# Up-projection's head: first unit's fifth product tied behind the second unit's third; a weight step, squares and down-projection's differences issued later

## The chip, the cores and the metric
One Trainium2 chip, one of its cores. The kernel is one launch; its metric is the device time of the core in microseconds, lower is better. The profile is of one execution; its span runs from the first to the last instruction.

## The reference
One layer of a decoder block in float32 on x of 1 x 2048 x 1024:

```python
h = rmsnorm(x, attn_norm)
z = h @ w_in                      # pool channels | q | k | v | gates
a = pool_mixer(u_pool, w_pool, pool_scale)
b = swa_sink_attention(q, k, v, sinks)      # window 128
x = x + (g_pool * a + g_attn * b) @ w_out
h = rmsnorm(x, ffn_norm)
up = causal_depthwise_conv(h @ w_up, conv_w, conv_b)   # 1024 -> 2 * 2816, width 3
gate, val = up[..., :D_FF], up[..., D_FF:]
x = x + (silu(gate) * val) @ w_down
```

The change lies in the last four lines and in the output projection's sums for the second norm.

## The kernel before
The sequence is worked in two chunks of 1024 tokens (c = 0, 1): input projection and mixer, output projection (`Out`, `out_blocks`), up-projection (`Up`, `up`), down-projection (`Down`).

A product of f32 accuracy is made of fp32r matmuls: each factor is split into a rounded part and the rest (a ScalarE cast, L362 for weights and L1068 for activations, then a VectorE subtraction, L363 and L1069), and three of the four cross products are summed. On top of that the large projections use a scheme of seven block products in place of eight, with sums of blocks as factors (S1 to S4 of the weights, T1 to T4 of the activations).

In the up-projection, a unit f (22 of them, `u0`, `u1`, `u2`, ...) makes 128 gate and 128 value channels by seven products, methods `one` to `seven`. Each is 12 matmuls of 128x512 (`product`, L1254) into a bank of PSUM. A unit's `x` bank ("f" tag for u0 and u1) takes products one, three, five, seven in turn: after three, ScalarE copies the bank away (`kept`, L1444); after five, VectorE adds it to an earlier copy and writes half of the values (L1470); after seven, ScalarE copies it out (L1478). So five must wait for the copy, and seven for the add, of its own unit. Products four and six use another bank ("t" or "a"), and an add (L1474) ends six. Then come the convolution (L1489 on ScalarE, two L1492 on VectorE), SiLU (L1503), the gate's product (L1504) and a store.

The head of `up` handles units 0 to 2 together, because the factors T1 to T4 are only being made then: `right_t3`, `right_b22`, `right_t4` each subtract (L1237, L1247 for T4) and split. A unit's weights come in four steps (`weights(f, n)`): the second step holds L379, L382 and L383, the fourth L390 and L391.

The order on each engine is the scheduler's, from priorities by the place in the code; each engine works its queue strictly in that order. `with tc.issue_after(ins):` puts what is issued inside it right behind the instruction `ins` in that order, on ScalarE, VectorE and the others as well. It adds no dependence.

`Out.final` ends an output block: `added` (L1320) adds the residual, ScalarE squares the row (L1335), and VectorE adds the square to a sum (L1339). `stats` sums these sums over the channels by matmuls with a column of ones (L655), for the second norm. `Down.run` works through steps P1 to P7; for P2 it takes a difference of the loaded activations (L1888).

Of the kernel before, what the change touches and what calls it, by code (L numbers as in the profile page):

```python
# [21 lines left out]
ALU = mybir.AluOpType  # L22
# [200 lines left out]
def block_kernel(ctx: ExitStack, tc: tile.TileContext, x, xT, pos, vec, qkn, w_poolT, w_pool, w_q, w_kv,  # L223
                 w_gp, w_ga, w_out, w_up, w_down, outT):
    nc = tc.nc
    V, G, A = nc.vector, nc.gpsimd, nc.scalar
# [205 lines left out]
    for _ in range(20):  # L432
        nc.tensor.matmul(idle[:, 0:512], identr, identr.unsqueeze(1).to_broadcast([P, 4, P]),
                         start=True, stop=True)
# [815 lines left out]
    def product(bank, a, b, first):  # L1250
        i = 0
        for k in range(4):
            for x, y in ((0, 0), (0, 1), (1, 0)):
                nc.tensor.matmul(bank, a[:, x, k, :], b[k // 2][:, y, k % 2, :],  # L1254
                                 start=(first and i == 0), stop=(i == 11),
                                 skip_group_check=True)
                i += 1

    class Out:


        def __init__(self, c):
            self.c, self.m, self.w, self.b, self.xs, self.raws = c, [], [], {}, {}, []
            self.accs = [[], []]

        def mix(self):
            j = 3 - len(self.m)
# [49 lines left out]

        def added(self, h, n, m, bank):
            x = self.xs[h, n][:, m]
            V.scalar_tensor_tensor(x, bank, 0.5, x, op0=ALU.mult, op1=ALU.add)  # L1320

        def residual(self, h, n):
            x = self.xs[h, n] = up_.tile([P, 4, 512], F32, "U")
            load(x, self.rest(h, n))

        def final(self, h, n, m, bank):
            self.added(h, n, m, bank)
            x = self.xs[h, n][:, m]
            accs = self.accs[n]
            if not accs:  # L1330
                accs.append(fp.tile([P, 512], F32, "F"))
                A.square(accs[0], x)
            else:
                sq = mp.tile([P, 512], F32, "M")
                A.square(sq, x)  # L1335
                if h == 1 - n == 0 and m == 3:
                    accs.append(sq)
                else:
                    V.tensor_add(accs[0], accs[0], sq)  # L1339
            A.dma_start(x2d[4 * h + m][:, n * 512:n * 512 + 512], x)  # L1340

        def pairs(self):
# [3 lines left out]
    def out_blocks(ob):  # L1346

        heads = [Kept(f) for f in PRE]

        def run(*a, **kw):  # L1350
            for _ in ob.mul(*a, **kw):
                pass

        s = ps2.tile([P, T], F32, "s")
        x = [ps.tile([P, 512], F32, t) for t in "at"]
        x = [s[:, 0:512], x[0], s[:, 512:T], x[1]]
        ob.weights()
        ob.mix()
        ob.residual(0, 0)
        run(0, x, True, True)  # L1360
        ob.split()
        ob.first(2)
        right_t1(ob.m, ob.b, None)
        ob.mix()
        for m in range(4):
            ob.added(0, 0, m, x[m])
        ob.weights()
        ob.first(3)
        y = [ps.tile([P, 512], F32, t) for t in "ffta"]
        run(1, y, True, True)  # L1370
        ob.split()
        t2s = right_t2(ob.m, ob.b, None)
        ob.weights()
        for m in range(4):
            ob.final(0, 0, m, y[m])
        for n in ob.mul(2, x):
            if n == 0:
                ob.split()
                right_t3(ob.m, ob.b)
                ob.weights()  # L1380
            if n % 2 == 1:
                ob.kept(0, 1, n // 2, x[n // 2])
        for n in ob.mul(3, x):
            if n == 0:
                ob.split()
                right_t4(ob.m, ob.b, t2s)
                ob.weights()
                ob.residual(1, 0)
            if n % 2 == 1:
                ob.kept(1, 1, n // 2, x[n // 2])  # L1390
        for n in ob.mul(4, x):
            if n == 0:
                ob.split()
                ob.weights()
                right_b22(ob.m, ob.b)
            if n % 2 == 1:
                ob.final(1, 0, n // 2, x[n // 2])
        norms, b = [], {}

        def stats(n):  # L1400
            rstd(ob.accs[n], r2[:, 4 * n:4 * n + 4])

        def whole(n):
            return spread(r2[:, 4 * n:4 * n + 4], None)

        for n in ob.mul(5, y, True):
            if n == 0:
                ob.split()
                stream.fetch(stream.used + 1)
                stream.part(stream.used + 1)  # L1410
            if n == 2:
                stats(0)
            if n == 4:
                pb = whole(0)
            if n % 2 == 1:
                ob.final(1, 1, n // 2, y[n // 2])
        xg = ob.pairs()
        for j in range(2):
            right_first(xg, b, j, pb)
        for n in ob.mul(6, y):  # L1420
            if n % 2 == 1:
                ob.final(0, 1, n // 2, y[n // 2])
            if n == 3:
                for f in range(2):
                    heads[f].fetch("A11", "A12")
                stream.ahead().step(1)
        for j in range(2, 4):
            right_first(xg, b, j, pb)
        return xg, b, [lambda: stats(1), lambda: whole(1)], heads
# [3 lines left out]
    class Up:  # L1433
# [3 lines left out]
            self.c, self.f, self.b, self.w = c, f, b, w  # L1437

        def mul(self, bank, x, y, first=False):
            product(bank, self.w.w[x], self.b[y], first)  # L1440

        def kept(self, bank):
            t = qp.tile([P, 512], F32, "Q")
# [55 lines left out]
        def gate(self, yg=None):  # L1499
            if yg is None:  # L1500
                yg = self.conv(self.f, self.ug)
            t = mp.tile([P, T], F32, "M")
            A.activation(t, yg, AF.Silu)  # L1503
            V.tensor_mul(t, t, self.yv)  # L1504
            load(actd[self.f], t)

    def up(c, xg, b, norms, heads, dn):
        units = [Up(c, f, b, heads[f] if f < 2 else None) for f in range(FT)]

        def weights(f, n):  # L1510
            if f < FT:
                if units[f].w is None:
                    units[f].w = stream.get("up", f)
                units[f].w.step(n)

        u0, u1, u2 = units[:3]
        u0.one()
        norms[0]()  # L1520
        u1.one()
        pb = norms[1]()
        u0.two()
        weights(2, 0)
        u2.one("t")
        for u in (u0, u1):
            u.w.fetch("S1", "S4")
        u0.w.fetch("S3", "S2")
        right_t1(xg, b, pb)
        u1.two()  # L1530
        u2.two()
        t2s = right_t2(xg, b, pb)
        u0.four()
        u0.w.fetch("A22")
        u1.w.fetch("A22")
        right_t3(xg, b, (right_t2.sub, right_t2.low))
        third = parted.low
        u1.four("a")
        u0.three()
        last = Up.last  # L1540
        u1.w.fetch("S3", "S2")
        u1.three()

        with tc.issue_after(last):
            right_b22(xg, b)
        u0.five()
        with tc.issue_after(third):
            right_t4(xg, b, t2s)
        weights(2, 1)
        u0.six()  # L1550
        yg = u0.conv(0, u0.ug)
        u1.five()
        u0.seven()
        u0.value()
        weights(2, 1)
        u0.gate(yg)
        weights(2, 1)
        for f in range(2, FT + 1):
            u = units[f] if f < FT else None
            old = units[f - 1]  # L1560
            if u and f > 2:
                u.one()
                u.two()
            if f >= FT - 1:
                dn.fetch(3)
            weights(f + 1, 1)
            if u is None:
                old.six()
                dn.make(2)
                yg = old.conv(old.f, old.ug)  # L1570
                old.seven()
                old.value()
                old.gate(yg)
                break
            old.seven()
            old.value()
            weights(f + 1, 1)
            u.three()
            if f == FT - 1:
                dn.make()  # L1580
                if c + 1 < NCH:
                    spread(r1[:, c + 1, :])
            weights(f + 1, 1)
            old.six()
            if f < FT - 1:
                old.gate()
            weights(f + 1, 1)
            u.four()
            u.five()
            if f == FT - 1:  # L1590
                old.gate()
            if c + 1 < NCH and FT - 10 <= f < FT - 2:
                squares(c + 1, f - (FT - 10), row(c + 1, f - (FT - 10), fp, "F"))
            if c + 1 < NCH and f == FT - 2:
                norm1(c + 1, 0, NB)
# [198 lines left out]
    class Down:  # L1794
# [80 lines left out]
        def run(self, extra):  # L1875

            gives = []
            for i, (g, p, k) in enumerate(self.steps):
# [6 lines left out]
                        self.loads += [(1, int(p == "P4"), k, h) for h in range(2)]  # L1885
                if p == "P2":
                    a = self.raw[g, 0, k]
                    V.tensor_sub(a[:, 0:4:2], a[:, 1:4:2], a[:, 0:4:2])  # L1888
                if k > 0 and gives:
                    gives.pop(0)()  # L1890
                self.make(i + 1 + self.AHEAD - self.made)
# [255 lines left out]
```

## Time and profile before
| | |
|---|---|
| time, median of 3 runs | 2384.95 us (2383.26 to 2388.49) |
| the profiled execution, its own time | 2385.3 us |
| its span | 2383.6 us |
| mean granted TensorE clock | 0.998 |
| units' head, chunk 0 | about 603 to 630 us |
| units' head, chunk 1 | about 1768 to 1795 us |
| sums for the second norm, chunk 1 | about 1714 to 1729 us |
| start of down-projection, chunk 0 | about 1004 us |

The prediction quotes rows of several views. In the timeline a row is: start, duration, engine, line, operation, out<-in, shape, count, and in brackets the time that the engine sat idle before it and what ended that. A window's row has its length, each engine's busy time with its count, the granted TensorE clock, the share of the DMA engines and GB/s.

### The profile page before, as it was taken

The page shows a single profiled execution, that of the slowest core. Times are in us where ns is not written, and L with a number is a line of the kernel's source. Part 1 is how long each engine was busy: PE and PEld are TensorE (multiplying, and loading weights), DVE is VectorE, ACT ScalarE, POOL GpSimd, SP SyncE. Part 2 cuts the span into 40 slices and gives each one's busy share as a digit, 9 for nine tenths or more (in the row PEclk, how much of TensorE's full clock was granted, in tenths as well). Part 3 has the DMA queues.
Part 4 walks back from the last instruction along what each step waited for, and adds up shares of the span by engine and source line. Part 5 has one row for each costly group of instructions (what it writes and reads, how often), then busy time and mean ns, then how long its engine had stood idle before and what let it go on. Part 6 is the DMA issues. An engine that isn't in the chain of part 4 may idle for free.

```text
span 2383.6 us, 30120 instructions
## 1 busy us (share of the span) xinstructions
PE 2356.7 (99%) x11040; PEld 1958.7 (82%) x11040; DVE 1906.5 (80%) x2907; ACT 1185.7 (50%) x2164; POOL 190.5 (8%) x142
## 2 busy tenths in 40 slices
PE   9999999999999999999999999999999999999999
PEld 8888888888788888888888888888788888888887
DVE  8688888977977777899955867788798777779994
ACT  7555455455654555643623544455445545554441
POOL 1123121010000000000002232200000000000000
PEclk9999999999999999999999999999999999999999
DMA  9768778697222233644454776666733222228421
GB/s 348 241 202 237 223 213 286 216 344 270 73 88 91 93 106 106 210 168 162 133 195 151 228 219 196 197 207 230 234 129 105 80 80 80 80 75 288 141 71 53
DMA packets 165060, 408.10 MB, mean 171 GB/s; under 512 B 14128, under 2 KB 50480, under 8 KB 155184
## 3 DMA queue, kind: packets, MB, share of 16 engines
q1 hardware_dynamic: 151616, 373.48, 46.6%
q0 software_dynamic: 8256, 24.12, 4.3%
q10 hardware_dynamic: 5040, 8.58, 1.0%
q8 instruction: 87, 1.43, 0.2%
q14 instruction: 61, 0.50, 0.1%
HBM read 267.32 MB, written 138.81 MB: 170 GB/s over the span
## 4 chain that ended last, share of the span: by engine, by line
PE 85%; DVE 8%; DMA 3%; ACT 2%; issue 1%; POOL 0%; SPq 0%; DVEq 0%; ACTq 0%; POOLq 0%
PE f L1254 22%; PE f L266 16%; PE t L1254 12%; PE a L1254 6%; PE f L1912 4%; PE a L1912 4%; PE s L1912 4%; PE t L1912 4%; PE f L1098 3%; PE a L959 2%; PE s L898 2%; PE a L266 2%; PE t L931 1%; DVE U L1069 1%; DMA U<-xd 1%
## 5 line engine op out<-in xcount | busy, mean ns | idle before, releaser
L266 PE MATMUL f<-U,U 128*128 128x512 f32 (+1 forms) x2088 | 490.2, 389 | 4.5 <-ACT U L249 2.1
L266 PEld LDWEIGHTS f<-U,U 128*128 128x128 f32 x2088 | 381.3, 189 | 81.3 <-ACT U L249 2.7
L1254 PE MATMUL f<-U,U 128*128 128x512 f32 x1872 | 445.1, 390 | 2.7 <-ACT Q L1444 2.5
L1254 PEld LDWEIGHTS f<-U,U 128*128 128x128 f32 x1872 | 350.8, 188 | 77.7 <-ACT Q L1444 3.8
L1492 DVE SCALAR_TENSOR_TENSOR M<-F,vc,M 128x1024 f32<-128x1024 f32 x176 | 225.3, 1282 | 139.0 <-ACT M L1489 138.7
L1254 PE MATMUL t<-U,U 128*128 128x512 f32 x1332 | 314.6, 389 | 0.0
L1254 PEld LDWEIGHTS t<-U,U 128*128 128x128 f32 x1332 | 249.7, 188 | 52.4 <-ACT Q L1444 0.3
L362 ACT CAST U<-R 128x1024 fp32r<-128x1024 f32 x147 | 153.6, 1053 | 82.0 <-DVE R L391 42.6
L1254 PE MATMUL a<-U,U 128*128 128x512 f32 x756 | 183.9, 390 | 0.7 <-ACT Q L1444 0.7
L363 DVE TENSOR_TENSOR U<-R,U 128x1024 fp32r<-128x1024 f32 x147 | 179.2, 1221 | 0.3 <-ACT U L362 0.3
L1254 PEld LDWEIGHTS a<-U,U 128*128 128x128 f32 x756 | 141.3, 188 | 30.2 <-ACT Q L1444 1.2
L1254 PE MATMUL f<-U,M 128*128 128x512 f32 x624 | 150.2, 389 | 0.3 <-DVE F L1470 0.3
L917 ACT ACTIVATE Q<-s,st,rq 128x128 f32<-128x128 f32 x256 | 113.8, 456 | 49.9 <-DVE st L914 49.7
L1254 PEld LDWEIGHTS f<-U,M 128*128 128x128 f32 x624 | 117.0, 188 | 25.0 <-DVE F L1470 0.8
L939 POOL TENSOR_SCALAR_AFFINE_SELECT M<-M 128x1024 fp32r<-128x1024 f32 x64 | 94.4, 1475 | 383.4 <-DVE st L919 230.4
L1870 ACT CAST U<-U 128x1024 fp32r<-128x1024 f32 x76 | 79.0, 1051 | 84.7 <-PE s L1912 22.2
L1478 ACT COPY F<-f 128x512 f32<-128x512 f32 x52 | 30.5, 586 | 182.2 <-PE f L1254 182.0
L1489 ACT ACTIVATE M<-F,vc 128x1024 f32<-128x1024 f32 x88 | 109.4, 1243 | 3.3 <-DVE F L1474 1.9
L1871 DVE TENSOR_TENSOR U<-U,U 128x1024 fp32r<-128x1024 f32 x76 | 92.0, 1219 | 2.7 <-ACT U L1870 2.5
L1870 ACT CAST F<-U 128x1024 fp32r<-128x1024 f32 x44 | 46.2, 1049 | 93.8 <-PE a L1912 62.5
L966 ACT COPY U<-a 128x512 f32<-128x512 f32 x64 | 37.5, 586 | 108.5 <-PE a L959 108.3
L1098 PE MATMUL f<-U,U 128*128 128x512 f32 x384 | 88.5, 390 | 0.3 <-DVE M L1104 0.2
(320 smaller groups left out, 4051.9 us busy)
## 6 DMA issues: line engine op xcount, KB each, us to landing
R<-w_up SPq DMA_DIRECT2D x80, 512.0 KB, 3.7
actd<-M SPq DMA_DIRECT2D x44, 512.0 KB, 2.7
U<-w_down SPq DMA_DIRECT2D x88, 256.0 KB, 5.0
U<-actd SPq DMA_DIRECT2D x88, 256.0 KB, 5.2
qd<-U SPq DMA_DIRECT2D x64, 256.0 KB, 3.8
Q<-qd SPq DMA_DIRECT2D x64, 256.0 KB, 4.7
R<-w_out SPq DMA_DIRECT2D x30, 512.0 KB, 4.5
U<-kept_S SPq DMA_DIRECT2D x12, 1024.0 KB, 7.9
```

The costliest lines, as they stand in the source:

```text
L266: nc.tensor.matmul(out, a, b, start=(i == 0), stop=(i == n - 1))
L362: A.copy(t[:, 0], raw)
L363: V.tensor_sub(t[:, 1], raw, t[:, 0].bitcast(F32))
L917: A.activation(pr[:, h, :], sc[:, h, 0:P], AF.Exp, bias=nm[:, h:h + 1], scale=it["rq"][:, h:h + 1], accum_out=rs[:, h:h + 1])
L939: G.affine_select(own.rearrange("p a h q -> p (a h) q"), pa.bitcast(F32).rearrange("p a h q -> p (a h) q"), pattern=[[0, 8], [1, P]], base ...
L1098: nc.tensor.matmul(po, w[:, a, k, :], ms[k // 2][n][:, b, k % 2, :], start=(first and i == 0), stop=(last and i + 1 == len(order)))
L1254: nc.tensor.matmul(bank, a[:, x, k, :], b[k // 2][:, y, k % 2, :], start=(first and i == 0), stop=(i == 11), skip_group_check=True)
L1489: A.activation(y, u[:, 2:], AF.Identity, bias=cw[:, 3, m:m + 1], scale=cw[:, 2, m:m + 1])
L1492: V.scalar_tensor_tensor(y, u[:, j:j + T], cw[:, j, m:m + 1], y, op0=ALU.mult, op1=ALU.add)
L1870: A.copy(hi, src)
L1871: V.tensor_sub(lo, src, hi.bitcast(F32))
L1912: nc.tensor.matmul(into[m], u[:, 0, c_], v[:, 1], start=(first and j == 0), stop=(k == n - 1 and j == 2), skip_group_check=True)
```

## The change
Five edits, all of them to the order of issue:
1. u0's fifth product, with its add, is issued after the end of u1's third (`Up.end`).
2. u0's sixth follows the end of u0's fifth, and u1's sixth (issued in the loop, f == 2) the end of u0's sixth.
3. The step of u2's weights that holds L382 moves into the block that is issued after T3's last subtraction, with T4.
4. In `Out.final` a square's add is issued after the next block's L1320; `stats` issues what is left first.
5. Down-projection's differences of P2 are issued after the last gate's product.

```diff
+                ins = nc.tensor.matmul(bank, a[:, x, k, :], b[k // 2][:, y, k % 2, :],
+                                       start=(first and i == 0), stop=(i == 11),
+                                       skip_group_check=True).ins
...
+        return ins
...
         def final(self, h, n, m, bank):
-            self.added(h, n, m, bank)
+            with tc.issue_after(self.added(h, n, m, bank)):
+                while self.sums:
+                    self.sums.pop()()
...
                 else:
-                    V.tensor_add(accs[0], accs[0], sq)
+                    self.sums.append(lambda: V.tensor_add(accs[0], accs[0], sq))
...
         def stats(n):
+            while ob.sums:
+                ob.sums.pop()()
             rstd(ob.accs[n], r2[:, 4 * n:4 * n + 4])
...
         def mul(self, bank, x, y, first=False):
-            product(bank, self.w.w[x], self.b[y], first)
+            Up.end = product(bank, self.w.w[x], self.b[y], first)
...
-            V.tensor_mul(t, t, self.yv)
+            Up.gated = V.tensor_mul(t, t, self.yv).ins
...
         with tc.issue_after(last):
             right_b22(xg, b)
-        u0.five()
+        with tc.issue_after(Up.end):
+            u0.five()
         with tc.issue_after(third):
             right_t4(xg, b, t2s)
-        weights(2, 1)
-        u0.six()
+            weights(2, 1)
+        with tc.issue_after(Up.end):
+            u0.six()
+        six = Up.end
         yg = u0.conv(0, u0.ug)
         u1.five()
         u0.seven()
...
-            old.six()
+            with tc.issue_after(six) if f == 2 else nullcontext():
+                old.six()
...
                 if p == "P2":
                     a = self.raw[g, 0, k]
-                    V.tensor_sub(a[:, 0:4:2], a[:, 1:4:2], a[:, 0:4:2])
+                    with tc.issue_after(Up.gated):
+                        V.tensor_sub(a[:, 0:4:2], a[:, 1:4:2], a[:, 0:4:2])
```

Lines of the changed code lie up to 6 higher in `Up` (L1450 is the old L1444, L1476 the old L1470, L1480 the old L1474, L1498 the old L1492), 2 to 4 higher in `Out`.

The order on TensorE, at the head of chunk 0. f_5626 is u0's bank, f_5654 u1's, t_5767 that of u0's sixth; the right-hand factors are in the right place of each name pair.

```order
 L1254 MATMUL f_5626<-U_5764,U_5715 128x512 x6
+L1254 MATMUL f_5654<-U_5758,U_5823 128x512 x6
+L1254 MATMUL f_5654<-U_5764,U_5823 128x512 x6
 L1254 MATMUL f_5626<-U_5787,U_5715 128x512 x6
 L1254 MATMUL f_5626<-U_5791,U_5715 128x512 x6
-L1254 MATMUL t_5767<-U_5839,U_5711 128x512
-L1254 MATMUL a_5794<-U_5839,U_5713 128x512
-L1254 MATMUL t_5767<-U_5839,U_5711 128x512
-L1254 MATMUL f_5654<-U_5758,U_5823 128x512 x6
-L1254 MATMUL f_5654<-U_5764,U_5823 128x512 x6
-L1254 MATMUL t_5767<-U_5839,U_5711 128x512 x4
+L1254 MATMUL t_5767<-U_5839,U_5711 128x512 x6
```

u1's third stands ahead of u0's fifth now, and u0's sixth behind it in one piece. A little later, between u0's and u1's seventh, three matmuls of u2's third are left where twelve of it and eight of u1's sixth stood.

ScalarE at the same place; Q_5837 is the copy of u1's bank after its third product, U_5861 and U_5865 the two halves of T4, U_5868 the first weights of u2 to be split.

```order
 L1068 CAST U_5861<-U_4893 128x1024
-L1487 COPY uh_195<-F_5845 128x2
-L1444 COPY Q_5837<-f_5654 128x512
 L1068 CAST U_5865<-U_4894 128x1024
+L1450 COPY Q_5837<-f_5654 128x512
 L362 CAST U_5868<-R_5539 128x1024
 L362 CAST U_5924<-R_5537 128x1024
+L1493 COPY uh_195<-F_5845 128x2
```

The copy of u1's bank has moved behind the cast of T4's second half.

VectorE at the same place, before; F_5845 is u0's add after its fifth, F_5889 u1's, U_4894 the difference L1247 of T4's second half:

```order
L1069 TENSOR_TENSOR U_5842<-U_4894,U_5842 128x1024
L1470 TENSOR_TENSOR F_5845<-f_5626,Q_5780 128x512
L1069 TENSOR_TENSOR U_5861<-U_4893,U_5861 128x1024
L1247 TENSOR_TENSOR U_4894<-U_4894,M_5762 128x2x512
L1069 TENSOR_TENSOR U_5865<-U_4894,U_5865 128x1024
L363 TENSOR_TENSOR U_5868<-R_5539,U_5868 128x1024
```

and in the change:

```order
L1069 TENSOR_TENSOR U_5842<-U_4894,U_5842 128x1024
L1069 TENSOR_TENSOR U_5861<-U_4893,U_5861 128x1024
L1247 TENSOR_TENSOR U_4894<-U_4894,M_5762 128x2x512
L1069 TENSOR_TENSOR U_5865<-U_4894,U_5865 128x1024
L363 TENSOR_TENSOR U_5868<-R_5539,U_5868 128x1024
L1476 TENSOR_TENSOR F_5845<-f_5626,Q_5780 128x512
L363 TENSOR_TENSOR U_5924<-R_5537,U_5924 128x1024
L1480 TENSOR_TENSOR F_5624<-t_5767,Q_5821 128x512
L382 TENSOR_TENSOR R_5581<-R_5579,R_5581 128x512
L363 TENSOR_TENSOR U_5935<-R_5579,U_5935 128x1024
L1498 SCALAR_TENSOR_TENSOR M_5885<-F_5624,vc_129,M_5885 128x1024 x2
L1476 TENSOR_TENSOR F_5889<-f_5654,Q_5807 128x512
```

u0's add has moved behind four pieces of T4 and weight work. u1's add stands behind both of u0's conv rows L1498 for the gate channels.

VectorE at the sums of chunk 1, before; U_14585 and U_14593 are the blocks that the residual is added to, F_14470 the sum of squares, M_14716 the last square:

```order
L1320 SCALAR_TENSOR_TENSOR U_14585<-s_14308,U_14585 128x512
L382 TENSOR_TENSOR R_14734<-R_14732,R_14734 128x512
L1339 TENSOR_TENSOR F_14470<-F_14470,M_14665 128x512
L1320 SCALAR_TENSOR_TENSOR U_14585<-a_14309,U_14585 128x512
L1339 TENSOR_TENSOR F_14470<-F_14470,M_14682 128x512
```

and in the change:

```order
L1322 SCALAR_TENSOR_TENSOR U_14584<-s_14308,U_14584 128x512
L1343 TENSOR_TENSOR F_14470<-F_14470,M_14484 128x512
L1322 SCALAR_TENSOR_TENSOR U_14584<-a_14309,U_14584 128x512
L1343 TENSOR_TENSOR F_14470<-F_14470,M_14665 128x512
L1322 SCALAR_TENSOR_TENSOR U_14584<-s_14308,U_14584 128x512
```

L382 is gone from this place, and each L1343 adds the square of one block earlier.

More of the change, by code (lines that the diff above doesn't have):

```diff
@@ L1253, in product @@
             for x, y in ((0, 0), (0, 1), (1, 0)):
-                nc.tensor.matmul(bank, a[:, x, k, :], b[k // 2][:, y, k % 2, :],
-                                 start=(first and i == 0), stop=(i == 11),
-                                 skip_group_check=True)
+                ins = nc.tensor.matmul(bank, a[:, x, k, :], b[k // 2][:, y, k % 2, :],
+                                       start=(first and i == 0), stop=(i == 11),
+                                       skip_group_check=True).ins
                 i += 1
+        return ins
     class Out:
@@ L1264, in __init__ @@
             self.accs = [[], []]
+            self.sums = []
         def mix(self):
@@ L1319, in added @@
             x = self.xs[h, n][:, m]
-            V.scalar_tensor_tensor(x, bank, 0.5, x, op0=ALU.mult, op1=ALU.add)
+            return V.scalar_tensor_tensor(x, bank, 0.5, x, op0=ALU.mult, op1=ALU.add).ins
         def residual(self, h, n):
```

## The prediction
> **What bounds the kernel now.** I read the page first, then the list of waits of TensorE, then the timeline at each place where the change moves something, and last a table of windows for the clock. From the page:
>
> ```profile
> span 2383.6 us, 30120 instructions
> ...
> PE 2356.7 (99%) x11040; PEld 1958.7 (82%) x11040; DVE 1906.5 (80%) x2907; ACT 1185.7 (50%) x2164; POOL 190.5 (8%) x142
> ```
>
> The tensor engine TensorE (PE) is busy 99% of the span, and the change adds or removes no matmul. So only two things can change the time: gaps between matmuls, and the granted clock. The list of waits gives the gaps it can reach:
>
> ```profile
> engine line waited for: us in total, times, longest us
> ...
> PE f L1254 <- ACT Q L1444: 2.5, 2, 1.3
> PE a L655 <- DVE F L1339: 2.2, 1, 2.2
> ```
>
> The first is the up-projection's head, once in each chunk: TensorE waits for ScalarE's copy of a bank. The second is the row sums of squares in chunk 1. Here is the head of chunk 0 on the three engines:
>
> ```profile
> 603.71 3.21 PE L1254 MATMUL f<-U,U 128*128 128x512 f32 x12
> ...
> 607.56 0.58 ACT L1444 COPY Q<-f 128x512 f32<-128x512 f32 x1
> 608.04 3.16 ACT L1068 CAST U<-U 128x1024 fp32r<-128x1024 f32 x3
> 608.20 3.04 PE L1254 MATMUL f<-U,U 128*128 128x512 f32 x12 [1.27 <-ACT Q L1444]
> 608.83 1.22 DVE L1247 TENSOR_TENSOR U<-U,M 128x1024 f32<-128x1024 f32 x1
> 609.97 2.35 DVE L1069 TENSOR_TENSOR U<-U,U 128x1024 fp32r<-128x1024 f32 x2
> ...
> 612.24 0.68 DVE L1470 TENSOR_TENSOR F<-f,Q 128x512 f32<-128x512 f32 x1
> ...
> 614.67 0.59 ACT L1444 COPY Q<-f 128x512 f32<-128x512 f32 x1 [1.52 <-PE f L1254]
> 615.23 1.05 ACT L1068 CAST U<-U 128x1024 fp32r<-128x1024 f32 x1
> ...
> 616.74 2.88 PE L1254 MATMUL f<-U,U 128*128 128x512 f32 x12
> 617.45 1.22 DVE L363 TENSOR_TENSOR U<-R,U 128x1024 fp32r<-128x1024 f32 x1
> ...
> 619.46 2.88 PE L1254 MATMUL f<-U,M 128*128 128x512 f32 x12
> ...
> 622.65 0.69 DVE L382 TENSOR_TENSOR R<-R,R 128x512 f32<-128x512 f32 x1
> ...
> 623.25 2.47 DVE L1492 SCALAR_TENSOR_TENSOR M<-F,vc,M 128x1024 f32<-128x1024 f32 x2
> ...
> 630.11 5.15 PE L1254 MATMUL t<-U,U 128*128 128x512 f32 x22
> ...
> 988.53 2.60 DVE L1492 SCALAR_TENSOR_TENSOR M<-F,vc,M 128x1024 f32<-128x1024 f32 x2 [2.12 <-ACT M L1489]
> ```
>
> A product of 12 matmuls takes 2.72 us from start to start (616.74 to 619.46). u0's third, at 603.71, would be followed at about 606.76 (1.44 ahead of 608.20, counting what the wait's record leaves out, and after 0.2 and 0.1 of smaller gaps). VectorE (DVE) works without a pause here: its subtractions of 128x1024 follow each other by 1.14 (608.83 to 609.97), those of 128x512 by 0.60 (622.65 to 623.25), and two L1492 of which the second reads the first take 2.60 (988.53). That decides what follows.
>
> **Part 1, the head of chunk 0.** u1's third now fills 606.76 to 609.48, u0's fifth runs to 612.20, u0's sixth to 614.92. The old wait is gone. But three results that TensorE needs next have moved back behind the T4 work on ScalarE and VectorE (the order rows under the change), and I walk them with the durations above.
> - *u1's fifth* needs ScalarE's copy of u1's bank. It now stands behind the cast of T4's second half, which waits for the second subtraction L1247. On VectorE that one comes after 609.97 + 3 x 1.13 = 613.37 and ends at 614.59; the cast ends 1.05 later, at 615.69 with 0.05 to hand over; the copy, which overlaps it by 0.1 and takes 0.58, ends at 616.18. TensorE starts at 616.24 instead of 614.92: **1.3** of wait. Before, ScalarE did this copy at 614.67, ahead of that cast.
> - *u0's seventh* could start at 616.24 + 2.72 = 618.96. It needs u0's add L1470, before at 612.24. Ahead of it now stand L1069 (from 615.73), a cast that takes the buffer which this L1069 releases (616.99 to 618.04), and L363 (618.08); the add runs 619.22 to 619.91. TensorE starts at 619.97: **1.0**.
> - *u1's seventh* has three filler matmuls ahead and could start at 619.97 + 2.72 + 0.68 = 623.37. It needs u1's add, behind L363 (1.14), L1474 (0.60), L382 (0.60), L363 (1.14) and two dependent L1492 (2.56 to 2.60): from 619.82 that is 625.86, and the add ends at 626.55. TensorE starts at 626.61: **3.2**.
> - Then u1's seventh, nine and twelve matmuls: 626.61 + 2.72 + 2.04 + 2.72 = 634.09 for u2's fourth, which stood at 630.11. **Chunk 0: +4.0.** Behind it nothing new is late: the second part of the order is the old one, and VectorE has 24 matmuls to catch up.
>
> **Chunk 1** has the same queue:
>
> ```profile
> 1768.54 2.99 PE L1254 MATMUL f<-U,U 128*128 128x512 f32 x12
> 1772.80 3.04 PE L1254 MATMUL f<-U,U 128*128 128x512 f32 x12 [1.27 <-ACT Q L1444]
> ```
>
> Its order puts weight steps between the T4 work, and I count from the end of the cast that u1's copy waits for. u1's fifth starts 0.55 later, with a wait of 1.4. For u0's seventh VectorE does L1069 (1.14), L383, L390 and L391 (0.68, 0.61, 0.60), L363 (1.14) and the add (0.69), which ends 4.90 after the cast; TensorE could start at 0.55 + 2.72 = 3.27: 1.7. For u1's seventh follow L363, L1474, L363, L382, the two L1492 and the add, 1.14 + 0.60 + 1.14 + 0.60 + 2.56 + 0.69 = 6.7, against one product and four filler matmuls, 2.72 + 0.91: 3.0 (L363 starts with the product, within 0.1). In all 6.1, for the 1.5 that goes: **+4.6**. If VectorE were not late, both heads would lose their waits, 1.6 + 1.5 = -3.1; that is the lower end of this term, and +8.6 the upper.
>
> **Parts 2 and 3, the squares and the weight step in chunk 1.**
>
> ```profile
> 1714.27 1.23 POOL L1316 DMA_DIRECT2D U<-xT  x1 [5.24 <-issue]
> ...
> 1716.34 0.69 DVE L382 TENSOR_TENSOR R<-R,R 128x512 f32<-128x512 f32 x1 [4.71 <-DMA R<-w_up]
> ...
> 1718.93 0.69 DVE L1339 TENSOR_TENSOR F<-F,M 128x512 f32<-128x512 f32 x1 [0.70 <-ACT M L1335]
> ...
> 1723.66 1.05 PE L655 MATMUL a<-one,F 128*128 128x1 f32 x8 [2.16 <-DVE F L1339]
> ...
> 1726.31 2.76 PE L1298 MATMUL t<-U,U 128*128 128x512 f32 x6
> ```
>
> ```profile
> U<-xT POOLq DMA_DIRECT2D x4, 512.0 KB, 6.3
> ```
>
> VectorE stood 4.71 us at L382 for a DMA, and then each add waited for its square in turn (0.70 each round). With L382 behind the T4 work and each square's add behind the next L1320, VectorE follows the banks as TensorE fills them (one each 2.72): the last add of these sums ends about 1721.4, when TensorE gets there. That takes away about 2.3. One bound is the residual that GpSimd orders at 1714.27: 6.3 later is 1720.6, where L1320 wants it at about 1720.1, so I take **-2.1**.
>
> **The clock.**
>
> ```profile
> core 0: us, PE busy (x) PEld busy (x) DVE busy (x) ACT busy (x) POOL busy (x), PEclk, DMA share, GB/s
> 350.20:353.60 3.40, 1.50 (x5) 0.86 (x5) 3.40 (x6) 3.40 (x6) 0.00 (x0) 0.99 0.02 8
> 353.60:357.00 3.40, 3.15 (x8) 2.51 (x9) 3.40 (x9) 2.10 (x10) 1.13 (x1) 0.50 0.84 264
> 606.10:609.50 3.40, 2.13 (x10) 1.43 (x9) 3.40 (x4) 2.89 (x4) 0.00 (x0) 1.00 0.00 0
> 609.50:612.90 3.40, 3.40 (x17) 2.79 (x16) 3.40 (x5) 1.60 (x2) 0.00 (x0) 1.00 0.02 5
> ...
> 1722.30:1725.70 3.40, 2.04 (x13) 1.87 (x14) 1.46 (x3) 1.48 (x5) 0.70 (x1) 1.00 0.92 346
> 1725.70:1729.10 3.40, 3.40 (x11) 2.51 (x10) 1.72 (x3) 0.63 (x1) 0.34 (x1) 0.50 0.98 298
> ```
>
> Twice in the span the granted clock is 0.50 for 3.4 us, each time right behind a stretch with little matmul: 1.50 and 2.04 busy. The old head wait left 2.13, and the clock stayed at 1.00. One such stretch costs half of 3.4, **1.7**. The one at 1725.7 goes with the wait ahead of it: -1.7. But a wait of 3.0 to 3.2 us leaves, wherever such a stretch begins, one with at most about 1.8 busy. I therefore expect half a clock behind the third wait of each head, +1.5 each, since part of the wait falls into the slow stretch: together **+1.3**.
> [...]
>
> **Part 4, down-projection.**
>
> ```profile
> 994.37 1.23 DVE L1888 TENSOR_TENSOR U<-U 128x1024 f32<-128x1024 f32 x1 [2.10 <-DMA U<-actd]
> ...
> 1001.45 3.01 PE L1254 MATMUL f<-U,M 128*128 128x512 f32 x12 [0.35 <-DVE F L1470]
> ...
> 1006.38 0.97 PE L1912 MATMUL f<-U 128*128 128x512 f32 x3 [0.56 <-ACT F L1478]
> ```
>
> At the end of chunk 0's up-projection VectorE stands 2.10 in front of a difference, L1888, until its operand lands, and TensorE then waits twice, 0.35 and 0.56 by the record, 1.2 with the matmuls' starts. The differences now come behind the last gate, so the add L1470 no longer stands behind them: **-1.2**. They are read only by down-projection's fourth group of steps, some 15 us later, which covers the delay; uncovered it would be one difference, 1.2. Chunk 1 has no wait there.
>
> **Sum** on the profiled 2385.3 (span 2383.6 and 1.7 around it; 0.35 above the median of the runs): +4.0 + 4.6 - 2.1 - 1.2 + 1.3 = +6.6, 2391.9; against the median, and rounded, **2391.6**.
>
> **Rivals.**
> - *The clock stays* behind the new waits. [...] Against: the two rows above. 2391.6 - 3.0 = **2388.6**.
> - *Half the waits*: ScalarE and VectorE work some 1 us ahead of my walk, each wait halves, and no clock drops. Heads 2.8 - 1.6 and 3.0 - 1.5, the rest -2.1 - 1.7 - 1.2: 2385.3 - 2.3 - 0.3 = **2382.7**. For it: a walk over twenty instructions adds its errors up. Against: each handover in it is a row's duration.
> - *The other side: faster.* VectorE gets ahead of TensorE, because u1's third in front gives it 2.72 us. It decides at u0's add: if that runs by 616, u0's seventh never waits and u1's add follows in time. Heads -3.1, sums -2.1, clock -1.7, down -1.2: -8.1, **2377**. Against it: VectorE is busy 3.40 of 3.40 in both windows of the old head, so 2.72 us of other matmuls create no room, and the order puts its adds later than before.
>
> **Chances.** Forecast 0.52 (one drop only would still be 2390); clock stays 0.20; half the waits 0.10; faster 0.13; worse than forecast 0.05 (the residual late, or the drop of chunk 1's squares staying too). The bounds of the unknown terms (0.5 on the squares, 0.7 on each head's walk, 1.7 on the clock) reach 2394; the lower end takes in the rival of the clock and that of half the waits, 2382. About 0.2% of the time, 4.8 us, is what a measurement of this kernel can tell from no change: below 2380.2 is faster, above 2389.7 slower. Faster 0.14, within 0.32, slower 0.54.
>
> **What would show it.** In the changed kernel's timeline: three waits of TensorE in each head (copy, u0's add, u1's add) near 1.3, 1.0 to 1.7 and 3.1; the record of L655 without a wait; no wait at the first row of L1912's kind; windows with clock 0.50 just behind u1's seventh. I am wrong if u1's add ends before TensorE wants it, or if the clock never drops in a head.

## The result, and the profile after

| | before | changed |
|---|---|---|
| median, same chip | 2384.46 us (6 runs, 2380.28 to 2388.49) | 2397.03 us (6 runs, 2391.52 to 2403.17) |
| ratio, 95% interval | | 1.0055 (1.0038 to 1.0071) |
| the profiled execution | 2385.3 us | 2400.55 us |
| a second series, with a second profile | 2384.21 us (17 runs) | 2394.63 us (4 runs), 1.0042 (1.0028 to 1.0056) |

The change makes the kernel slower: by 0.55% in the first series and by 0.42% in the second. The direction was forecast; the size was not: 2391.6 with a range up to 2394 was given.

The engines' busy times from the page of the changed kernel, and its list of waits of TensorE (in all, times, longest):

```profile
PE 2362.6 (98%) x11040; PEld 1962.7 (82%) x11040; DVE 1907.3 (80%) x2907; ACT 1185.5 (49%) x2164; POOL 190.3 (8%) x142
```

```profile
PE f L1254 <- DVE F L1476: 10.0, 4, 4.7
...
PE a L655 <- DVE F L1343: 2.5, 1, 2.5
PE f L1254 <- ACT Q L1450: 2.4, 2, 1.2
```

TensorE has the same number of matmuls. A new first row stands in the list: 10.0 us for VectorE's adds of the fifth products, in four waits. The other two rows have nearly the numbers of before, but they are other waits: the copy waited for is now that of u1's bank, no longer that of u0's, and the wait at L655 is at a later place, as will be seen.

The head of chunk 0, and the three waiting products of chunk 1, in the changed kernel's timeline:

```profile
603.20 8.66 PE L1254 MATMUL f<-U,U 128*128 128x512 f32 x36
...
615.13 0.58 ACT L1450 COPY Q<-f 128x512 f32<-128x512 f32 x1
...
615.76 3.04 PE L1254 MATMUL f<-U,U 128*128 128x512 f32 x12 [1.18 <-ACT Q L1450]
...
618.74 0.68 DVE L1476 TENSOR_TENSOR F<-f,Q 128x512 f32<-128x512 f32 x1
...
619.48 3.01 PE L1254 MATMUL f<-U,M 128*128 128x512 f32 x12 [0.68 <-DVE F L1476]
...
622.64 0.69 DVE L382 TENSOR_TENSOR R<-R,R 128x512 f32<-128x512 f32 x1 [1.49 <-DMA R<-w_up]
...
627.08 0.69 DVE L1476 TENSOR_TENSOR F<-f,Q 128x512 f32<-128x512 f32 x1
...
627.83 4.60 PE L1254 MATMUL f<-U,M 128*128 128x512 f32 x12 [4.66 <-DVE F L1476]
...
637.03 3.33 PE L1254 MATMUL t<-U,U 128*128 128x512 f32 x14
...
1788.18 3.02 PE L1254 MATMUL f<-U,U 128*128 128x512 f32 x12 [1.19 <-ACT Q L1450]
...
1792.62 3.03 PE L1254 MATMUL f<-U,M 128*128 128x512 f32 x12 [1.42 <-DVE F L1476]
...
1799.83 5.49 PE L1254 MATMUL f<-U,M 128*128 128x512 f32 x12 [3.27 <-DVE F L1476]
```

The three waits of each head are there, for the three instructions that the prediction names. The second is a little shorter than forecast, and the third of chunk 0 is 4.66 by its record, 4.8 counted from the starts of the matmuls: 1.6 more than the 3.2 forecast. The reason stands a few rows above it: VectorE stood 1.49 us at L382 for a load. The product behind the wait lasts 4.60 in place of 2.9, which is the clock. The windows show it:

```profile
624.71:628.12 3.41, 0.29 (x1) 0.29 (x2) 2.92 (x3) 0.94 (x4) 0.00 (x0) 1.00 0.00 0
628.12:631.53 3.41, 3.41 (x9) 2.68 (x9) 2.26 (x2) 3.38 (x3) 0.00 (x0) 0.50 0.00 0
1747.70:1751.11 3.41, 1.14 (x6) 0.60 (x4) 3.41 (x5) 1.99 (x3) 0.00 (x0) 1.00 1.01 339
1751.11:1754.52 3.41, 3.17 (x15) 3.20 (x16) 1.41 (x3) 1.75 (x4) 0.00 (x0) 0.50 0.98 372
1754.52:1757.93 3.41, 3.41 (x10) 2.73 (x11) 1.72 (x3) 0.17 (x1) 1.01 (x1) 0.50 0.90 317
1795.48:1798.90 3.42, 1.08 (x5) 0.56 (x3) 3.10 (x3) 0.10 (x1) 0.00 (x0) 1.00 0.44 144
1798.90:1802.31 3.41, 2.48 (x6) 2.00 (x7) 2.03 (x3) 3.19 (x4) 0.00 (x0) 0.50 0.00 0
1802.31:1805.72 3.41, 3.41 (x10) 2.64 (x9) 2.54 (x3) 1.43 (x3) 0.00 (x0) 0.50 0.00 0
```

The clock drops behind the third wait of each head, as forecast, but in chunk 1 it stays down for two windows, and for two more it drops at 1751, where nothing was forecast. That makes five windows of 3.41 at half clock, at up to 1.7 each (a little less in the two in which TensorE was busy for only 3.17 and 2.48); the kernel before had two such windows. What happened ahead of 1751:

```profile
1713.81 1.23 POOL L1318 DMA_DIRECT2D U<-xT  x1 [8.68 <-ACT U L1284]
...
1723.17 1.23 POOL L1318 DMA_DIRECT2D U<-xT  x1 [8.14 <-issue]
...
1723.92 1.47 SPq L243 DMA_DIRECT2D U<-kept_A  x2
...
1736.73 0.69 DVE L1322 SCALAR_TENSOR_TENSOR U<-t,U 128x512 f32<-128x512 f32 x1 [4.18 <-DMA U<-xT]
...
1751.35 0.56 PE L655 MATMUL a<-one,F 128*128 128x1 f32 x2 [2.51 <-DVE F L1343]
```

The norm's sums are taken twice in a chunk, once for each half of the columns. The first (1727.05) had no wait left, as forecast. The second waits 2.51 here: VectorE stood 4.18 for the last piece of the residual, which GpSimd ordered at 1723.17 and which landed 13 us later, beside two loads of 1024 KB that SyncE ordered at 1723.92.

### The profile page after: what moved, and what is told of

It is laid out like the page before. It is cut to its first block, busy times and chain, and to the rows that moved or that the text cites. A ratio compares the mean times of both kernels' runs of the same rounds, so it can differ in the third digit from the quotient of the medians.

```text
span 2398.8 us, 30131 instructions
## 1 busy us (share of the span) xinstructions
PE 2362.6 (98%) x11040; PEld 1962.7 (82%) x11040; DVE 1907.3 (80%) x2907; ACT 1185.5 (49%) x2164; POOL 190.3 (8%) x142
## 4 chain that ended last, share of the span: by engine, by line
PE 85%; DVE 9%; DMA 2%; ACT 2%; issue 1%; POOL 0%; DVEq 0%; SPq 0%; ACTq 0%; POOLq 0%
PE f L1254 22%; PE f L266 16%; PE t L1254 12%; PE a L1254 6%; PE f L1923 4%; PE a L1923 4%; PE s L1923 4%; PE t L1923 4%; PE f L1098 3%; PE a L959 2%; PE s L898 2%; PE a L266 2%; DVE U L1069 1%; PE t L931 1%; PE s L1300 1%
## 5 line engine op out<-in xcount | busy, mean ns | idle before, releaser
L1498 DVE SCALAR_TENSOR_TENSOR M<-F,vc,M 128x1024 f32<-128x1024 f32 x176 | 225.6, 1282 | 151.9 <-ACT M L1495 151.2
```

The lines of the kernel that those rows point to most:

```text
L1498: V.scalar_tensor_tensor(y, u[:, j:j + T], cw[:, j, m:m + 1], y, op0=ALU.mult, op1=ALU.add)
```

## The experiments

Each ran beside the kernel before on the same chip; the first four share runs of before (median 2384.56 us, 25 runs), the other four as well (2384.21 us, 17 runs). "Parts" are the five edits of the change. One sentence of the text ahead has to be put right first: a tie acts on the engine of the instruction that is named, not on all. `issue_after(Up.end)` holds matmuls; the adds and copies were not tied, and moved because the scheduler put other work of their engines first.

**Parts 1 and 2 alone**

```diff
-        u0.five()
+        with tc.issue_after(Up.end):
+            u0.five()
...
-        u0.six()
+        with tc.issue_after(u0.end5):
+            u0.six()
+        six = Up.end
...
-            old.six()
+            with tc.issue_after(six) if f == 2 else nullcontext():
+                old.six()
```

> Only parts 1 and 2 of the change (u0's fifth behind u1's third, the sixths tied), all else as before. Theory (the ties alone bring the adds and the copy behind T4 and weight work): three waits of TensorE in each head, about 1.3, 0.9 and 4.7 in chunk 0 (the third with L382's wait for its load, 1.5), about 1.4, 1.6 and 3.0 to 3.4 in chunk 1, half clock behind the third; the old wait of 2.2 at L655 for the first sums stays, none at the second L655. Time 8 to 12 us above before, about 2394. Rival (the loss comes from the moved weight step and the squares): the third wait of chunk 0 stays under 3.3 without a wait at L382, and the time lies within 5 us of before.

Measured: 2399.48 us, ratio 1.0058 (1.0041 to 1.0075). Its waits:

```profile
PE f L1254 <- DVE F L1471: 11.3, 5, 4.6
...
PE f L1254 <- ACT Q L1445: 1.7, 2, 1.1
...
PE a L655 <- DVE F L1340: 0.9, 1, 0.9
```

Two rows of its timeline:

```profile
623.19 0.69 DVE L382 TENSOR_TENSOR R<-R,R 128x512 f32<-128x512 f32 x1 [1.38 <-DMA R<-w_up]
...
1738.20 0.69 DVE L1321 SCALAR_TENSOR_TENSOR U<-t,U 128x512 f32<-128x512 f32 x1 [3.60 <-DMA U<-xT]
```

The two head ties alone cost 15 us, which is all of the loss and more than the 8 to 12 expected. L382 waits for its load ahead of u1's add in chunk 0 without part 3, too, so part 3 didn't bring it there. The second half of the expectation failed: the wait at the first sums, which was to stay without part 4, had gone (VectorE stood 1.82 at L382 there, where it had stood 4.71), and two waits of 0.9 stood at the second sums, where none was expected. VectorE stood 3.60 for the late residual here too, so the order of the squares isn't needed for that.

**Parts 4 and 5 alone, and parts 3 to 5**

```diff
             with tc.issue_after(self.added(h, n, m, bank)):
                 while self.sums:
                     self.sums.pop()()
...
                     with tc.issue_after(Up.gated):
                         V.tensor_sub(a[:, 0:4:2], a[:, 1:4:2], a[:, 0:4:2])
```

> Only parts 4 and 5 (squares' adds one block later, down-projection's differences behind the last gate); the head and the weight step as before. Theory: head waits as before (one of 1.3 in each chunk), down-projection's two waits gone (-1.2), L655's first wait smaller than before's 2.2. If the residual's transfer collides with other loads because of part 4's order, a second L655 wait of about 2.5 with half clock shows here too, and the time is 2384 to 2388; if it needs the head's delay or the moved weight step, there is none and the time is about 2380.

> Parts 3, 4 and 5, without the head's ties. Theory: as e2, with L382 out of the squares of chunk 1, so the first L655 wait is under 0.5 and no half clock stands behind it: 2379 to 2381 if the second L655 does not wait, 2384 to 2387 if it does. The second L655 wait here but not in e2 would put it on the moved weight step; in both, on the squares; in neither, on the ties or on chance. Rival (parts 3 to 5 gain nothing): the time equals before within 1 us.

Measured: 2380.20 us, ratio 0.9986 (0.9977 to 0.9995), and with part 3 2380.40, 0.9989 (0.9979 to 0.9998). Of the waits that the change is concerned with, parts 4 and 5 leave only the old ones of the heads:

```profile
PE f L1254 <- ACT Q L1450: 2.5, 2, 1.3
```

So squares and differences gain some 4 us, close to the 2.1 + 1.2 + 1.7 (clock behind the first sums) forecast for them. Part 3 adds nothing that can be measured to that. With parts 4 and 5 alone VectorE still stands 3.64 us at L382 for its load in that stretch, but the adds of the squares then catch up before TensorE asks for the sum.

**The ties, with the adds held in front** (parts 1, 2, 4, 5; T4's second subtraction behind u0's add, u1's fifth behind u0's sixth)

```diff
-            right_t4(xg, b, t2s)
-            weights(2, 1)
+            right_t4(xg, b, t2s, sum0)
+        weights(2, 1)
...
-        u1.five()
+        with tc.issue_after(six):
+            u1.five()
```

> Parts 1, 2, 4 and 5, and one more tie: T4's second subtraction L1247 is issued behind u0's add L1470, and u1's fifth behind u0's sixth. The order then has u0's add ahead of T4's second half, u1's copy ahead of its cast, and fourteen filler matmuls between the sevenths. Theory (the loss is the late copy and adds, not u1's third in front): chunk 0's head keeps at most one wait of 0.5, chunk 1's has 0.9 and 2.1; no half clock in chunk 0. Time about 2380 to 2384. Rival (u1's third in front costs by itself, whatever the adds do): waits in chunk 0 of over 3 in all and a time above 2390.

Measured: 2381.78 us, ratio 0.9991 (0.9981 to 1.0000). The waits for the adds:

```profile
PE f L1255 <- DVE F L1477: 2.1, 2, 1.8
...
PE f L1255 <- DVE U L1069: 0.7, 1, 0.7
```

The time lies in the 2380 to 2384 expected, and chunk 0's head keeps one wait, of 0.33. So u1's third product in front need not cost much: with u0's add ahead of T4's second half again, and more matmuls between the sevenths, 15 us shrink to 1.6 over parts 4 and 5 alone. The loss comes from where adds and copy stand relative to the products that need them. This run doesn't part the two remedies: it puts the adds earlier in VectorE's order, and it also has fourteen matmuls between the sevenths where the changed kernel has three, which alone give u1's add 2.5 us more (11 x 2.72 / 12).

**The changed kernel once more**

> The changed kernel once more, unaltered, for a second profile. Theory A (the residual's second half lands late by the order of the transfers itself): the second row sums of squares in chunk 1 wait about 2.5 us for VectorE's add again, the last of GpSimd's residual transfers is issued over 9 us after the one before, and two stretches of half clock follow. Theory B (chance of one execution): that transfer is issued 6 to 7 us after the one before, there is no such wait, and the profiled time is about 6 us lower than the first profile's 2400.55. Either way the three waits of chunk 0's head stay within 0.3 of 1.3, 0.8 and 4.8. Median 2395 to 2399.

Measured: 2394.63 us, just under the 2395 to 2399 expected; profiled execution 2394.95. Rows of its timeline and windows:

```profile
628.42 4.61 PE L1254 MATMUL f<-U,M 128*128 128x512 f32 x12 [4.65 <-DVE F L1476]
...
1714.84 1.23 POOL L1318 DMA_DIRECT2D U<-xT  x1 [8.44 <-DMA R<-wo_g]
...
1723.45 1.23 POOL L1318 DMA_DIRECT2D U<-xT  x1 [7.38 <-ACT M L1339]
...
1733.86 0.69 DVE L1322 SCALAR_TENSOR_TENSOR U<-t,U 128x512 f32<-128x512 f32 x1
...
1750.00 0.28 PE L655 MATMUL a<-one,F 128*128 128x1 f32 x2
```

```profile
1792.81:1796.22 3.41, 0.89 (x4) 0.76 (x5) 2.33 (x3) 1.62 (x3) 0.00 (x0) 1.00 0.05 18
1796.22:1799.63 3.41, 3.41 (x10) 2.63 (x9) 2.84 (x3) 2.64 (x3) 0.00 (x0) 0.50 0.00 0
```

Theory B holds in the main: the heads' waits are the same within 0.03 (1.35, 0.82, 4.82 in chunk 0, counted from matmul starts), but no wait stands at the second sums, and the clock drops for one window behind each head. So 5.6 us of the first profile's loss belonged to that execution. Theory B's detail was wrong: the last order went out 8.6 us after the one before, not 6 to 7. What differed was the landing. In the first profile the order's packets start at 1728.46, after those of the two loads from kept_A (1725.42), and end at 1736.22; here they start at 1725.39, ahead of the loads' (1729.24), and end at 1730.24. In these two profiles the transfer whose packets came first was done first; why the order of the packets differs isn't shown.

**The residual in four orders** (chunk 1's last two quarters)

```diff
-            if m % 2 == 1:
-                m = slice(m - 1, m + 1)
+            one = h == self.c == 1
+            if m % 2 == 1 or one:
+                m = slice(m if one else m - 1, m + 1)
                 G.dma_start(x[:, m], self.rest(h, n)[:, m], accum_op=ALU.add)
```

> The changed kernel; only in chunk 1, the residual of the last two 512-column quarters is added by four orders of 256 KB from GpSimd, one for each bank, where there were two of 512 KB. Theory (each 512 KB order waits until the one before has landed): with quarters the last order goes out at about 1716 to 1718 instead of 1723.2, all has landed by about 1727, the second row sums of squares wait less than 0.7 us and the two half-clock stretches behind them go: 5 to 6 us below the changed kernel, about 2391. Rival (the loads from SyncE take the DMA engines, whoever is issued when): the last quarter lands after 1733 still, the wait stays above 1.5 us, and the time is within 2 us of the changed kernel's.

Measured: 2397.40 us, ratio 1.0050 (1.0037 to 1.0064).

```profile
1714.63 1.75 POOL L1319 DMA_DIRECT2D U<-xT  x2 [7.78 <-ACT U L1284]
1718.09 0.88 POOL L1319 DMA_DIRECT2D U<-xT  x1 [1.71 <-ACT U L1315]
...
1719.09 3.03 PE L1300 MATMUL s<-U,U 128*128 128x512 f32 x12 [1.46 <-DVE U L1323]
...
1750.64 0.28 PE L655 MATMUL a<-one,F 128*128 128x1 f32 x2
```

The mechanism held and the gain did not come. The last order goes out at 1718.09, as expected, its packets have ended at 1725.53, and the second sums have no wait. But the time is no lower than the changed kernel's two medians, 2397.03 and 2394.63: another wait, 1.46 at the bank of L1300, stands where the changed kernel had 0.3 to 0.6, since a weight load from wo_g came later, and in this profile chunk 0's head took two windows at half clock. How often the late residual strikes in unprofiled runs isn't known; this run doesn't show that it sets the median.

**The fourth weight step later** (what VectorE does of it held behind u1's add)

```diff
+        sum1 = Up.sum
         u0.seven()
         u0.value()
-        weights(2, 1)
+        with tc.issue_after(sum1):
+            weights(2, 1)
```

> The changed kernel; only VectorE's and, through it, ScalarE's work of unit 2's fourth weight step is held behind unit 1's add in the up-projection's head. That takes L363, L382 (which stood 1.49 us for its load in the changed kernel) and L390 from between unit 0's add and unit 1's. By durations alone the waits of chunk 0's head become 0.6, 1.0 and 2.3, those of chunk 1 1.4, 0.5 and 3.8. If the third wait of chunk 0 was 4.8 because of L382's wait for its load, it falls to 2.3, chunk 0 gains 3.0 to 3.5 and its half-clock stretch may go too (another 1.7). If it was 4.8 because VectorE's queue is slower than the sum of its durations, it falls by the removed work alone, to about 3.9, and chunk 0 gains about 2. Median 2391 to 2394 by the first, 2394 to 2396 by the second.

Measured: 2392.23 us, ratio 1.0030 (1.0018 to 1.0042). Timeline of the head of chunk 0, and windows:

```profile
620.60 0.69 DVE L1476 TENSOR_TENSOR F<-f,Q 128x512 f32<-128x512 f32 x1
...
623.29 2.61 DVE L1498 SCALAR_TENSOR_TENSOR M<-F,vc,M 128x1024 f32<-128x1024 f32 x2 [1.41 <-ACT M L1495]
626.00 0.69 DVE L1476 TENSOR_TENSOR F<-f,Q 128x512 f32<-128x512 f32 x1
...
626.75 3.04 PE L1254 MATMUL f<-U,M 128*128 128x512 f32 x12 [2.16 <-DVE F L1476]
```

```profile
622.82:626.24 3.42, 1.77 (x8) 1.13 (x6) 2.81 (x3) 0.69 (x3) 0.00 (x0) 1.00 0.00 0
626.24:629.65 3.41, 2.90 (x13) 2.38 (x14) 3.15 (x5) 3.27 (x5) 0.00 (x0) 1.00 0.18 36
1786.77:1790.18 3.41, 1.38 (x7) 0.80 (x5) 2.81 (x3) 1.07 (x1) 0.00 (x0) 1.00 0.52 154
1790.18:1793.59 3.41, 1.28 (x3) 1.09 (x4) 3.16 (x5) 1.99 (x4) 0.00 (x0) 0.50 0.00 0
1793.59:1797.00 3.41, 3.41 (x9) 2.65 (x9) 3.17 (x3) 2.27 (x2) 0.00 (x0) 0.50 0.45 154
```

The third wait fell from 4.8 to 2.3, not to 3.9: it was L382's wait for its load. With it went chunk 0's half clock. Chunk 1's third wait grew to 4.3, with two windows at half clock, which took part of the gain back: 2.4 us against the changed kernel's 2394.63. (The first wait was expected at 0.6 and stayed at 1.34: the walk was 0.7 off there.)

**An order meant to beat both** (the kernel of the ties with the adds in front, and three more ties)

```diff
-        weights(2, 1)
+        with tc.issue_after(sum1):
+            weights(2, 1)
...
-            weights(f + 1, 1)
+            with tc.issue_after(sum1) if f == 2 else nullcontext():
+                weights(f + 1, 1)
...
-            old.seven()
+            if f == 2:
+                u.three()
+            with tc.issue_after(Up.end) if f == 2 else nullcontext():
+                old.seven()
```

> A version meant to beat both: unit 1's third product in front as in the changed kernel, with parts 4 and 5 (squares, differences), but VectorE's adds not left behind: T4's second subtraction is held behind unit 0's add, unit 1's fifth product comes behind unit 0's sixth, the weight steps of units 2 and 3 come behind unit 1's add, and unit 2's third product comes ahead of unit 1's seventh. By the durations of VectorE's and ScalarE's rows the waits are 0.5 in chunk 0's head and 0.2, 0.5 and 0.9 in chunk 1's, and 0.4 before the first row sums; no wait reaches the 2 us behind which the clock dropped. Against the kernel with parts 4 and 5 alone (2380.2, waits of 1.4 in each head) that is 0.9 less in chunk 0 and 0 to 0.5 more in chunk 1: 2379 to 2381, ratio to before 0.998 to 0.999. Rival (the late adds hurt wherever unit 1's third comes first): a wait over 2 us in a head, 2384 or more.

Measured: 2380.27 us, ratio 0.9986 (0.9977 to 0.9995). Its waits for adds, where the changed kernel's list has 10.0:

```profile
PE f L1255 <- DVE F L1477: 0.8, 2, 0.5
...
PE t L1255 <- DVE F L1477: 0.6, 1, 0.6
```

The heads are nearly free of waits: 0.7 in chunk 0, and the largest of chunk 1 is 0.7. It beats both kernels, by 4 us the one before. But so does the kernel with parts 4 and 5 alone, by the same 4 us with the old heads: the two can't be told apart.

## Why the prediction was right or wrong

- **What bounds it**: right. But for less than 1 us, all of the time that moved is found in gaps of TensorE and in its clock.
- **The head of chunk 0, +4.0**: the mechanism was right, a size wrong, and this is the first of two steps that failed. From 603.71 to 630.11 the head took 26.40 us before; in both profiles of the changed kernel it takes 33.83 (603.20 to 637.03 in the first), of which 1.7 is clock: +5.7. The first two waits were 1.3 and 0.8 (1.3 and 1.0 forecast), the third 4.8 (3.2 forecast). In the third, "L382 (0.60)" was counted as 0.60 of work. Its row of before had no idle time, but there it stood at 622.65; the changed order brings VectorE to it at 621.15, and the load it reads allows 622.64. In the trace of before that load's last completion signal came at 622.33, 0.3 ahead of L382: a row without a wait says that its input was there at that time, not that it is there earlier. The fourth weight step held back took the load out of the path, and the wait fell to 2.3.
- **The head of chunk 1, +4.6**: 1.35, 1.6 and 3.4, against 1.5 before: +4.9. Right.
- **Squares, -2.1**: the first sums' wait went, -2.3. The bound on it was read from the wrong row. GpSimd's order at 1714.27 is not read by the L1320 at 1720.1: in the code the blocks of the first sums get their residual by a load from SyncE, and GpSimd's last order belongs to the third block of the second sums (L1320 at 1731.04 in the trace of before, the row that stood 4.18 in the first profile). There the residual came 13.05 after its order in one profile of the changed kernel and 6.8 in the other. The first cost 2.5 and two windows at half clock, at a place that the prediction didn't look at: its chance of 0.05 for a late residual was too low and its 0.5 too small.
- **Part 3**, which the prediction priced together with the squares, added nothing of its own where it was tried, without the head's ties. With them it may: the third wait of chunk 1 is 4.55 by its record in the run of parts 1 and 2, and 3.27 in the changed kernel, but these two differ in parts 4 and 5 as well.
- **Down-projection, -1.2**: right; its first products start without a wait.
- **The clock, +1.3**: right in kind (a drop behind the third wait of each head, none behind the first sums), but far too low in size, and this is the second step that failed: it counted one window at most behind each head and none elsewhere. The first profile has five windows at half clock where the one of before has two, some 5 us more; the second has three, 1.7 more. The granted clock listed for single executions (to 0.001) says the same without a profile. Its mean is 0.9967 over the six executions of the first series, 0.9973 over the four of the second, and 0.9990 over the 42 of the kernel before that have it listed. By an estimate from these (the difference times 2390 us) the clock cost 5.5 us in the first series and some 4 in the second. It also accounts for the spread in size: the fastest of the six, 2391.52, has a clock of 0.999, the slowest, 2403.17, one of 0.994, and 0.005 of 2397 is 12 us, where 11.65 lie between them.

The account closes on the second profile: +5.7 + 4.9 - 2.3 - 1.2 and +1.7 of clock (two drops new, one gone) are +8.8, measured 2394.95 - 2385.3 = +9.65; 0.85 is not assigned. On the first come the second sums: 2.5 of wait, 3.4 of clock, and 1.7 for chunk 1's second window. Less the 1.7 of a half-clock window at 352 us that the second profile has and the first has not, that is 5.9, for a difference of 5.6. On the median of the first series, +12.6, the estimate of 5.5 for the clock leaves 7.1 for waits, where 5.3 was forecast; 1.6 of the difference is L382's load.

The rivals fell: the clock didn't stay, the waits weren't halved, and VectorE never got ahead. A faster order with u1's third in front did exist, but it needed the adds tied ahead and more matmuls between the sevenths, and it gained 4 us, not the 8.1 of that rival.

Every drop that is not cut off by the end of the span lasts 3.41 us or twice that: 3.41 at 353.56 and 1725.71 in the trace of before and at 628.12 in the first profile of the changed kernel, 6.83 at 1751.11 and 1798.90 there. The windows ahead of these had 0.29 to 2.05 us of matmul, so no limit on the busy time can be read from them alone: in the rows of the later fourth step a window with 1.38 is followed by half clock, one with 1.77 isn't.

## What to carry to other kernels

When a reordering brings an instruction forward, look up when its loaded operand lands, not only how long it takes: a row without idle time can hide a load that arrived just in time, as L382's did by 0.3 us. When one engine is tied to a new order, write out what the scheduler makes of the other engines' queues; here the ties held matmuls, and the cost came from adds and copies that nobody had tied; the two kernels that tied those as well, with more matmuls to cover them, were no slower than the kernel before. And in these traces a wait of 2 to 5 us on TensorE cost up to 1.7 or 3.4 more in the clock, not always the same in two executions, so price the clock as a range, and compare the granted clocks of all executions before explaining a difference by one profile.

## What the runs showed that was not expected

- The half clock twice lasted two windows in the first profile. The stretch from 1798.90 to 1802.31 had 2.48 busy at half clock, and the next was still at 0.50. A drop can also come and go far from any change: the one at about 352 us stands in seven of the ten profiles, with both orders of the head; in the window from 350.20 TensorE was busy for 1.50 before, with half clock behind it, and for 1.57 in the first profile of the changed kernel, with full clock behind it. How little matmul brings a drop isn't shown: the drop of the kernel before at 1725.7 followed a window with 2.04 busy, though that figure holds thirteen matmuls of which eight have one column each.
- GpSimd's 512 KB residual orders went out one at a time: the next one's record starts 0.64 to 0.68 us after the last packet of the one before, in three traces (before: 1713.63 to 1714.27; changed: 1722.49 to 1723.17; again: 1722.78 to 1723.45). With orders of 256 KB two followed each other at once (two in 1.75 us from 1714.63). What makes it wait wasn't tried.
- The same 512 KB took 6.1 us from order to last packet before, 6.8 and 13.05 in the two profiles of the changed kernel.
